# A hybrid decoder step on one core: three edits around the token mixer, and the inner norm sums in two rounded parts

## The chip, the cores and the metric

The kernel runs on one core of a Trainium2 chip. The metric is the device time in microseconds (us) of one execution. Before the change the median of three runs is 2332.24 us (2332.10 to 2332.31).

## What is computed

One decoder layer over 256 prompt tokens and 8 x 4 = 32 sample tokens, 288 columns together, with 2048 features. Everything is float32.

```
h = h + 1/2 SwiGLU(RMSNorm(h))                      # FFN 1, 5632 hidden features
h = h + W_out [ norm(conv group) | norm(attention group) ]
h = h + 1/2 SwiGLU(RMSNorm(h))                      # FFN 2
h = h + sigmoid(W_g RMSNorm(h)) * (W_p p)           # per-layer embedding
y = RMSNorm(h)
attention: softmax(q k^T / sqrt(d) + F_t - F_s, causal) v,  F = running sum of log sigmoid(w_f x + b_f)
```

Attention has 8 heads of 128. The sample tokens attend to 1024 past tokens each, read from a paged cache through a table, and to the new tokens of their own sequence; F runs on over past and new tokens.

## The kernel before

**Products.** The residual `h` lies transposed in SBUF, 128 features by 288 tokens a tile, 16 tiles. A product of float32 quality is made of three products in float32r: the activation is split into a rounded part and the rest (`xh`, `xl`, made by `x_split` and `make_x` through `split`, L194: ScalarE rounds, L195, VectorE subtracts, L196), the weights as well (`whi`, `wlo`, `split_upto`, L263: ScalarE L271, VectorE L272), and TensorE adds hi x hi, hi x lo and lo x hi in one bank of PSUM (`pair`, lines 304, 305, 306). A chunk (a piece of a `pair`) is 512 KB of weights, split in two halves, and 24 products of 128 x 288. The pool of split halves holds five (`HALVES`), the pool of raw weights eight (`RAW`).

**Order.** The source writes a list of steps. A scheduler in the language's layer then chooses the order in which each engine gets its instructions; some are pinned with `keep_in_program_order`. Each engine takes its instructions from its list, one after the other. Weights are loaded on SP's queue (L234 to L237), the cache's pages on POOL's. `defer(fn, chunks)` puts work on a list that is run in the middle of a chunk, so many chunks later.

**Start.** The first two `pair`s (gate and up of FFN 1) are interleaved chunk by chunk, and `first` (L426) splits the activations just ahead of them: features 0, 1, then 2, 3, then 4 to 7 and so on. The loads stand in this order on SP: activations 0 and 1, the first gate weights in two parts, activations 2 and 3, the first up weights, and so on alternately; behind all 16 activation tiles and four gate and four up chunks comes `consts` (L471), which holds among others the identity, masks and the matrix `mean` (all entries 1/2048).

**Norms.** The squares of `h` are added in `acc` (L209 to L215). `norm_scale` (L190) defers `inv_rms` (L175), which multiplies `mean` by `acc` on TensorE in plain float32 (L180), so that each partition holds the mean, and makes the inverse root on ScalarE and VectorE. It is used six times: behind FFN 1's first chunks, for the mixer, for the two groups of the mixer, for FFN 2 and for the embedding; `finish` calls `inv_rms` once more at the end.

**Running sums of the new tokens.** `f_natural` (L555) turns the log forget values. `f_new` (L566) makes the running sums of the 32 new tokens from two products (L568, L569), `f_turn` turns them (L576), `f_rows` (L581) spreads them to 128 rows by a product (L583); each is deferred by a chunk.

**Sample attention.** `k_scores` (L667) is a unit of 16 small products on column tiles (L684); there are 16 units, one every three pieces. `new_scores` (L695) makes the scores of the new tokens, 16 products of 32 columns for each half of the sequences (L699). The pieces are numbered by `at` (L952): unit n stands at 1 + 3n, the two `new_scores` at 20 and 21. `sample_out` (L750) sums the value products of one half under a mask on VectorE (L762, L764) and defers `sample_turn` (L767) by two chunks, which transposes the sum on TensorE (L770).

Of the kernel before, what the change touches and what calls it, by code (L numbers as in the profile page):

```python
# [16 lines left out]
F32 = mybir.dt.float32  # L17
F32R = mybir.dt.float32r
I32 = mybir.dt.int32
AF = mybir.ActivationFunctionType  # L20
ALU = mybir.AluOpType
# [4 lines left out]
P = 128  # L26
# [4 lines left out]
DT = 4  # L31
NS = DB * DT
NT = SEQ + NS
DFF = 5632
NH = 8
# [26 lines left out]
def constants():  # L62

    rows = np.arange(P)
    hc, b, half, t = rows // 32, rows % 32 // 8, rows % 8 // 4, rows % 4
    h = 4 * half + hc
    parts = []

    def put(name, a):
        a = np.asarray(a, np.float32)  # L70
        full = np.zeros((P, a.shape[1]), np.float32)
        full[: a.shape[0]] = a
        at = sum(x.shape[1] for x in parts)
        CONST_COLS[name] = (a.shape[0], at, at + a.shape[1])
        parts.append(full)

    put("ident", np.eye(P))
    put("ones", np.ones((P, 1)))
    put("mean", np.full((P, P), 1.0 / D))
    put("iota", rows[:, None])  # L80
    put("headmask", (rows % 8 // 4 * 4 + rows % 32 // 8)[:, None] == np.arange(NH)[None])
    put("tri", np.where(np.arange(P)[None] <= rows[:, None], 0.0, NEG))
    cb, ct = np.arange(NS) // DT, np.arange(NS) % DT
    for g in range(2):
        own = (cb[None] == (b + 4 * g)[:, None])
        put(f"newmask{g}", np.where(own & (ct[None] <= t[:, None]), 0.0, NEG))
        put(f"newself{g}", own & (ct[None] == t[:, None]))
    put("fold", rows[:, None] % 32 == np.arange(NH)[None])
    put("tri32", (cb[:, None] == cb[None]) & (ct[:, None] <= ct[None]))
    pb, pg = np.arange(64) // PAGES, np.arange(64) % PAGES  # L90
    put("tri64", (pb[:, None] == pb[None]) & (pg[:, None] < pg[None]))
    put("sel64", pb[:, None] == cb[None])
    put("headsel", np.arange(NH)[:, None] == h[None])
    return np.concatenate(parts, 1)


def build(nc, tc, ctx, A, O):
# [3 lines left out]
    v, s, g, pe, sy = nc.vector, nc.scalar, nc.gpsimd, nc.tensor, nc.sync  # L101

    cst = pool("cst")
# [14 lines left out]
    def ktbank():  # L118

        names = [n for n in spare["tags"] for _ in range(BANKS[n])]  # L120
        spare["at"] += 1
        n = names[spare["at"] % len(names)]
        return bank(n, BANKS[n])
# [5 lines left out]
    def const(name):  # L129
        r, a, b = CONST_COLS[name]  # L130
        return C[:r, a:b]
# [7 lines left out]
    at = 0  # L139
# [32 lines left out]
    def log_tables():  # L172
        tc.keep_in_program_order(s.preload_act_table_set("natural_log_exp_and_others"))

    def inv_rms(out, parts, width, load=True):  # L175

        b = ktbank()
        m = b[:, :NT]
        for i, x in enumerate(parts):
            pe.matmul(m, const("mean"), x, start=i == 0, stop=i == len(parts) - 1)  # L180
        if load:
            log_tables()
        c = float(D // width)
        s.activation(ra, m, AF.Ln, bias=eps, scale=c)
        s.activation(out, ra, AF.Exp, scale=-0.5)
        v.scalar_tensor_tensor(ra, out, -0.5 * c, out, ALU.mult, ALU.mult)
        v.scalar_tensor_tensor(ra, m, EPS / c, ra, ALU.add, ALU.mult)
        v.scalar_tensor_tensor(out, ra, 1.5, out, ALU.add, ALU.mult)

    def norm_scale(out, squares, width, chunks):  # L190

        defer(lambda: inv_rms(out, [squares], width), chunks)

    def split(hi, lo, x, gcol):  # L194
        return (s.activation(hi, x, AF.Copy, scale=gcol),  # L195
# [138 lines left out]
    def defer(fn, chunks=1):  # L334

        deferred.append((state["chunk"] + chunks, fn))
# [132 lines left out]
        load_upto(2 * c + 2)  # L469
    items.clear()  # L470
    tc.keep_in_program_order(sy.dma_start(C, A["consts"]))  # L471


    M = {}
# [80 lines left out]
    def f_natural(lf, FT):  # L555
        fp = W["fp"][0]
        np_ = ktbank()
        nat = cst.tile([P, 40], F32, name="nat")
        for j in range(2):
            pe.transpose(np_[:, 16 + j * NH:16 + j * NH + NH], FT[:, j * P:j * P + P], ident[:NH, :NH])  # L560
        pe.transpose(np_[:NS, 32:40], lf[:, SEQ:], ident[:NH, :NH])
        v.tensor_copy(nat[:, 16:32], np_[:, 16:32])
        v.tensor_copy(nat[:NS, 32:40], np_[:NS, 32:40])
        M["nat"] = nat

        def f_new():  # L566
            pn = ktbank()
            pe.matmul(pn[:NS, :NH], const("tri32"), nat[:NS, 32:40], start=True, stop=False)  # L568
            pe.matmul(pn[:NS, :NH], const("sel64"), M["tot"], start=False, stop=True)  # L569
            Fn = fp.tile([NS, NH], F32, name="Fn")  # L570
            v.tensor_copy(Fn, pn[:NS, :NH])
            defer(lambda: f_turn(Fn))

        def f_turn(Fn):
            pt = ktbank()
            pe.transpose(pt[:NH, :NS], Fn, ident[:NS, :NS])  # L576
            FnT = fp.tile([NH, NS], F32, name="FnT")
            v.tensor_copy(FnT, pt[:NH, :NS])
            defer(lambda: f_rows(FnT))

        def f_rows(FnT):  # L581
            px = ktbank()
            pe.matmul(px[:, :NS], const("headsel"), FnT, start=True, stop=True)  # L583
            Fx = fp.tile([P, NS], F32, name="Fx")
            v.tensor_copy(Fx, px[:, :NS])
            M["newbias"], M["Fq"] = [], []
            for gi in range(2):
                nb = cst.tile([P, NS], F32, name=f"nbias{gi}")
                v.tensor_tensor(nb, const(f"newmask{gi}"), Fx, ALU.subtract)
                d = fp.tile([P, NS], F32, name=f"fd{gi}")  # L590
                v.tensor_tensor(d, Fx, const(f"newself{gi}"), ALU.mult)
                fq = cst.tile([P, 1], F32, name=f"fq{gi}")
                v.tensor_reduce(fq, d, AX.X, ALU.add)
                M["newbias"].append(nb)
                M["Fq"].append(fq)

        defer(f_new)
# [97 lines left out]
    def new_scores(gi):  # L695
        sc = ktbank()
        for half in range(2):
            for c in range(4):
                pe.matmul(sc[32 * c:32 * c + 32, :NS], M["qn"][gi][:, 4 * half + c, :], k_[4 * half + c][:, SEQ:],  # L699
                          start=half == 0, stop=half == 1, tile_position=(0, 32 * c))  # L700
        v.scalar_tensor_tensor(M["s", gi][:, PAGES * P:], sc[:, :NS], M["Fq"][gi], M["newbias"][gi], ALU.add, ALU.add)
# [48 lines left out]
    def sample_out(gi):  # L750
        mx = W["vv"][0]
        for b in range(4):
            for e in range(2):
                rows = slice(NS * e, NS * e + NS)
                pe.matmul(M["va", gi][e][32 * b:32 * b + 32, :], M["pv", gi][rows, 8, b], M["vs"][rows], start=False, stop=True,
                          tile_position=(NS * e, 32 * b))
        o = mx.tile([P, P], F32, name="so", tag="so", bufs=2)
        for hh in range(NH):
            src = M["va", gi][hh // 4][:, hh % 4 * P:hh % 4 * P + P]
            m = const("headmask")[:, hh:hh + 1]  # L760
            if hh == 0:
                v.tensor_scalar(o, src, m, None, ALU.mult)  # L762
            else:
                v.scalar_tensor_tensor(o, src, m, o, ALU.mult, ALU.add)  # L764
        defer(lambda: sample_turn(gi, o), 2)

    def sample_turn(gi, o):  # L767
        mx = W["vv"][0]
        t = ktbank()
        pe.transpose(t[:, :P], o, ident)  # L770
        for half in range(2):
            v.tensor_copy(M["oS"][:, 4 * half:4 * half + 4, 16 * gi:16 * gi + 16].rearrange("p c (b t) -> p c b t", t=DT),
                          t[:, :P].rearrange("p (b c a t) -> p a c b t", c=4, a=2, t=DT)[:, half])
        if gi == 1:
            s.dma_start(O["v_prompt"].rearrange("(j p) c -> p j c", p=P), M["vn"])
            for e in range(2):
                s.dma_start(O["v_sample"][:, 512 * e:512 * e + 512], M["vs"][NS * e:NS * e + NS])
            for hh in range(NH):
                split(za[hh][0][:, SEQ:], za[hh][1][:, SEQ:], M["oS"][:, hh, :], gain("norm_attn_out", hh))
            sq = mx.tile([P, NH, NS], F32, name="sqS")  # L780
            s.activation(sq, M["oS"], AF.Square)
            v.tensor_reduce(acc[:, SEQ:], sq.rearrange("p h n -> p n h"), AX.X, ALU.add)
# [169 lines left out]
    def at(i, *fns):  # L952
        marks.setdefault(i, []).extend(fns)
# [31 lines left out]
        fill += pair(A["w_out"], ob * 256, list(range(8)), lambda k: zc[k], out_conv(ob), late=1 if ob == 0 else 0)  # L985
    for n in range(16):
        at(1 + KSTEP * n, units[n] if n > 1 else units[n][1])
    at(20, lambda: new_scores(0))
    at(21, lambda: new_scores(1))
    at(27, lambda: softmax(0))  # L990
    at(49, lambda: softmax(1))
    at(48, v_start)
# [144 lines left out]
```

## Time and profile before

| | |
|---|---|
| median of the runs shown | 2332.24 us |
| span of the profiled execution, first to last instruction (its own time is not listed apart) | 2332.0 us |
| instructions in it | 44271 |
| VectorE busy | 57% |
| ScalarE busy | 45% |
| mean DMA rate | 190 GB/s |
| granted TensorE clock, mean | 0.998 |

In the rows of the profile PE is TensorE's products, PEld its weight loads, DVE VectorE, ACT ScalarE, POOL GpSimd, SP SyncE, and a q behind a name is the engine's sequencer. A timeline row gives the start in us, the length in us, engine, line, operation, output <- inputs, count, and in brackets how long the engine was idle before it and what ended that. Consecutive like instructions are merged in a row. Each float32 product of L180, and most others in float32, stands as two records. Matmul ends are modelled and overlap the next one's start, so spacing is read from starts.

### The profile page before, as it was taken

The page shows a single profiled execution, that of the slowest core. Times are in us where ns is not written, and L with a number is a line of the kernel's source. Part 1 is how long each engine was busy: PE and PEld are TensorE (multiplying, and loading weights), DVE is VectorE, ACT ScalarE, POOL GpSimd, SP SyncE. Part 2 cuts the span into 40 slices and gives each one's busy share as a digit, 9 for nine tenths or more (in the row PEclk, how much of TensorE's full clock was granted, in tenths as well). Part 3 has the DMA queues.
Part 4 walks back from the last instruction along what each step waited for, and adds up shares of the span by engine and source line. Part 5 has one row for each costly group of instructions (what it writes and reads, how often), then busy time and mean ns, then how long its engine had stood idle before and what let it go on. Part 6 is the DMA issues. An engine that isn't in the chain of part 4 may idle for free.

```text
span 2332.0 us, 44271 instructions
## 1 busy us (share of the span) xinstructions
PE 2316.4 (99%) x17390; PEld 2254.6 (97%) x17390; DVE 1338.6 (57%) x2395; ACT 1056.0 (45%) x1859; POOL 328.2 (14%) x401
## 2 busy tenths in 40 slices
PE   9999999999999999999999999999999999999997
PEld 9999999999999999888888999999999999999997
DVE  6555555555555575456466765555555555555755
ACT  7444444444444453334345554444434444444654
POOL 2010000000000013444445210000000000000110
PEclk9999999999999999999999999999999999999999
DMA  8575555545555457998988554545555555555452
GB/s 272 162 241 163 165 169 164 164 164 167 167 163 163 163 161 224 333 313 268 322 306 296 167 165 154 174 158 175 163 164 164 170 163 163 164 167 167 161 169 88
DMA packets 391137, 443.52 MB, mean 190 GB/s; under 512 B 17120, under 2 KB 371824, under 8 KB 390928
## 3 DMA queue, kind: packets, MB, share of 16 engines
q1 hardware_dynamic: 369456, 366.89, 49.3%
q0 software_dynamic: 20384, 71.38, 8.8%
q8 instruction: 136, 2.23, 0.4%
q10 hardware_dynamic: 1088, 2.42, 0.3%
q14 instruction: 73, 0.60, 0.1%
HBM read 435.56 MB, written 5.07 MB: 189 GB/s over the span
## 4 chain that ended last, share of the span: by engine, by line
PE 99%; DVE 0%; DMA 0%; ACT 0%; SPq 0%; issue 0%; DVEq 0%
PE mm L304 31%; PE mm L306 31%; PE mm L305 30%; PE va L742 1%; PE va L684 1%; PE va L304 1%; PE va L306 1%; PE va L305 1%; DMA h<-in_x_dram 0%; DVE h L1072 0%; PE kt L304 0%; PE kt L306 0%; PE kt L305 0%; PE kt L180 0%; PE kt L796 0%; PE kt L829 0%
## 5 line engine op out<-in xcount | busy, mean ns | idle before, releaser
L272 DVE TENSOR_TENSOR wlo<-wraw,whi 128x512 fp32r<-128x512 f32 x1384 | 972.0, 706 | 805.2 <-ACT whi L271 753.2
L271 ACT ACTIVATE whi<-wraw 128x512 fp32r<-128x512 f32 x1384 | 865.3, 630 | 938.5 <-PE mm L305 866.0
L304 PE MATMUL mm<-xh,whi 128*128 128x288 f32 x3680 | 1094.9, 298 | 0.0
L305 PE MATMUL mm<-xl,whi 128*128 128x288 f32 x3680 | 1085.6, 295 | 0.0
L306 PE MATMUL mm<-xh,wlo 128*128 128x288 f32 x3680 | 1082.0, 294 | 0.0
L304 PEld LDWEIGHTS mm<-xh,whi 128*128 128x128 f32 x3680 | 689.7, 187 | 23.2 <-issue 19.4
L306 PEld LDWEIGHTS mm<-xh,wlo 128*128 128x128 f32 x3680 | 692.9, 188 | 0.1
L305 PEld LDWEIGHTS mm<-xl,whi 128*128 128x128 f32 x3680 | 691.0, 188 | 0.2
L304 PE MATMUL mm<-hh,whi 128*128 128x288 f32 x1408 | 416.8, 296 | 0.0
L305 PE MATMUL mm<-hl,whi 128*128 128x288 f32 x1408 | 415.4, 295 | 0.0
L306 PE MATMUL mm<-hh,wlo 128*128 128x288 f32 x1408 | 414.0, 294 | 0.0
L370 POOL TENSOR_TENSOR sr<-sg,rs 128x288 f32<-128x288 f32 x88 | 72.3, 822 | 1409.2 <-ACT sg L368 1409.1
L306 PEld LDWEIGHTS mm<-hh,wlo 128*128 128x128 f32 x1408 | 265.2, 188 | 0.0
L305 PEld LDWEIGHTS mm<-hl,whi 128*128 128x128 f32 x1408 | 264.4, 188 | 0.0
L304 PEld LDWEIGHTS mm<-hh,whi 128*128 128x128 f32 x1408 | 263.8, 187 | 0.0
L390 DVE SCALAR_TENSOR_TENSOR h<-mm,h 128x288 f32<-128x288 f32 x192 | 87.1, 455 | 23.4 <-PE mm L306 23.0
L215 POOL TENSOR_TENSOR acc<-acc,sq 128x288 f32<-128x288 f32 x59 | 51.0, 865 | 248.5 <-ACT sq L214 245.6
L368 ACT ACTIVATE sg<-tg 128x288 f32<-128x288 f32 x88 | 39.1, 444 | 99.9 <-DVE tg L366 96.7
L243 POOL DMA_INDIRECT KT<-in_cache_k_dram,idx x64 | 65.0, 1015 | 122.9 <-PE va L684 54.6
L377 ACT ACTIVATE hh<-hd 128x288 fp32r<-128x288 f32 x88 | 39.2, 446 | 92.8 <-DVE hd L375 92.8
L247 POOL DMA_INDIRECT page<-in_cache_v_dram,idx x64 | 64.7, 1010 | 72.6 <-PE va L742 50.6
L378 DVE TENSOR_TENSOR hl<-hd,hh 128x288 fp32r<-128x288 f32 x88 | 40.7, 464 | 22.0 <-ACT hh L377 22.0
(231 smaller groups left out, 1319.4 us busy)
## 6 DMA issues: line engine op xcount, KB each, us to landing
wraw<-in_w_ffn_up_dram SPq DMA_DIRECT2D x176, 512.0 KB
wraw<-in_w_ffn_gate_dram SPq DMA_DIRECT2D x175, 512.0 KB
wraw<-in_w_ffn_down_dram SPq DMA_DIRECT2D x160, 512.0 KB
wraw<-in_w_in_dram SPq DMA_DIRECT2D x96, 512.0 KB
wraw<-in_w_out_dram SPq DMA_DIRECT2D x32, 512.0 KB
wraw<-in_w_ple_gate_dram SPq DMA_DIRECT2D x32, 512.0 KB
wraw<-in_w_ffn_down_dram SPq DMA_DIRECT2D x32, 256.0 KB
wraw<-in_w_ple_proj_dram SPq DMA_DIRECT2D x8, 256.0 KB
```

The source lines that it names most:

```text
L215: (v if k >= KT - last_on_v else g).tensor_tensor(acc, acc, sq, ALU.add)
L243: g.indirect_dma_start(out=t[:, i].rearrange("p h s -> p (h s)"), out_offset=None, in_=it["src"], in_offset=bass.IndirectOffsetOnAxis(ap=r ...
L247: g.indirect_dma_start(out=t, out_offset=None, in_=it["src"], in_offset=bass.IndirectOffsetOnAxis(ap=it["rows"], axis=0))
L271: s.activation(hi, x, AF.Copy)
L272: v.tensor_tensor(lo, x, hi.bitcast(F32), ALU.subtract)
L304: pe.matmul(o, hi[:, j % 2, w], xh, start=f, stop=False)
L305: pe.matmul(o, hi[:, j % 2, w], xl, start=False, stop=False)
L306: pe.matmul(o, lo[:, j % 2, w], xh, start=False, stop=l)
L370: g.tensor_tensor(r, u, rs, ALU.mult)
L377: s.activation(H["hi"][:, k, :], t, AF.Copy)
L378: v.tensor_tensor(H["lo"][:, k, :], t, H["hi"][:, k, :].bitcast(F32), ALU.subtract)
L390: v.scalar_tensor_tensor(h[:, k, :], o, 0.5, h[:, k, :], ALU.mult, ALU.add)
```

## The change

1. `sample_turn` of the first half is deferred by four chunks instead of two.
2. Both `new_scores` stand at piece 22, behind key unit 7 (1 + 3 x 7 = 22).
3. The new tokens' running sums and their spreading become one product: the totals of the past pages and the new tokens' values are written, spread to 128 columns, in one tile `E` of 96 rows (four VectorE copies), and multiplied by one constant matrix `newsum` of 96 x 32. Three matrices go out of `consts`, which shrinks from 786 to 626 columns.
4. `norm_scale` rounds the sum of squares on ScalarE (`sqh`), makes the rest on VectorE (`sql`) and defers two float32r products with `meanr`, a rounded copy of `mean`. The copy is made once, by a VectorE instruction that stands in the source behind the load of `consts`. The last norm, in `finish`, is as before.

```diff
+    meanr = cst.tile([P, P], F32R, name="meanr")
+    sqh, sql = (cst.tile([P, NT], F32R, name=f"sq{x}") for x in "hl")
+
-    def inv_rms(out, parts, width, load=True):
+    def inv_rms(out, parts, width, load=True, weights=const("mean")):
...
-            pe.matmul(m, const("mean"), x, start=i == 0, stop=i == len(parts) - 1)
+            pe.matmul(m, weights, x, start=i == 0, stop=i == len(parts) - 1)
...
     def norm_scale(out, squares, width, chunks):
-        defer(lambda: inv_rms(out, [squares], width), chunks)
+        s.activation(sqh, squares, AF.Copy)
+        v.tensor_tensor(sql, squares, sqh.bitcast(F32), ALU.subtract)
+        defer(lambda: inv_rms(out, [sqh, sql], width, weights=meanr), chunks)
...
     tc.keep_in_program_order(sy.dma_start(C, A["consts"]))
+    v.tensor_copy(meanr, const("mean"))
...
+        def spread(rows, src):
+            for a in range(2):
+                v.tensor_copy(E[rows].rearrange("p (c b a t) -> p c b a t", c=4, b=4, a=2)[:, :, :, a],
+                              src[:, 4 * a:4 * a + 4].unsqueeze(2).unsqueeze(3).to_broadcast([src.shape[0], 4, 4, DT]))
+        E = fp.tile([96, P], F32, name="sums")
+        spread(slice(0, 64), M["tot"])
+        spread(slice(64, 96), nat[:NS, 32:40])
         def f_new():
-            pn = ktbank()
-            pe.matmul(pn[:NS, :NH], const("tri32"), nat[:NS, 32:40], start=True, stop=False)
-            pe.matmul(pn[:NS, :NH], const("sel64"), M["tot"], start=False, stop=True)
-            Fn = fp.tile([NS, NH], F32, name="Fn")
-            v.tensor_copy(Fn, pn[:NS, :NH])
-            defer(lambda: f_turn(Fn))
-        def f_turn(Fn):
...
-        def f_rows(FnT):
             px = ktbank()
-            pe.matmul(px[:, :NS], const("headsel"), FnT, start=True, stop=True)
+            pe.matmul(px[:, :NS], E, const("newsum"), start=True, stop=True)
...
-        defer(lambda: sample_turn(gi, o), 2)
+        defer(lambda: sample_turn(gi, o), 4 if gi == 0 else 2)
...
-    at(20, lambda: new_scores(0))
-    at(21, lambda: new_scores(1))
+    at(22, lambda: new_scores(0), lambda: new_scores(1))
```

More of the change, by code (lines that the diff above doesn't have):

```diff
@@ L64, in constants @@
     rows = np.arange(P)
-    hc, b, half, t = rows // 32, rows % 32 // 8, rows % 8 // 4, rows % 4
-    h = 4 * half + hc
+    b, t = rows % 32 // 8, rows % 4
     parts = []
@@ L88, in constants @@
     put("fold", rows[:, None] % 32 == np.arange(NH)[None])
-    put("tri32", (cb[:, None] == cb[None]) & (ct[:, None] <= ct[None]))
     pb, pg = np.arange(64) // PAGES, np.arange(64) % PAGES
     put("tri64", (pb[:, None] == pb[None]) & (pg[:, None] < pg[None]))
-    put("sel64", pb[:, None] == cb[None])
-    put("headsel", np.arange(NH)[:, None] == h[None])
+    put("newsum", np.concatenate([pb[:, None] == cb[None], (cb[:, None] == cb[None]) & (ct[:, None] <= ct[None])]))
     return np.concatenate(parts, 1)
@@ L564, in f_natural @@
         M["nat"] = nat
-        def f_new():
-            pn = ktbank()
-            pe.matmul(pn[:NS, :NH], const("tri32"), nat[:NS, 32:40], start=True, stop=False)
-            pe.matmul(pn[:NS, :NH], const("sel64"), M["tot"], start=False, stop=True)
-            Fn = fp.tile([NS, NH], F32, name="Fn")
-            v.tensor_copy(Fn, pn[:NS, :NH])
-            defer(lambda: f_turn(Fn))
-        def f_turn(Fn):
[L575 to L579, printed above, removed]
-        def f_rows(FnT):
+        def spread(rows, src):
[5 more added lines that the diff above has]
+        spread(slice(64, 96), nat[:NS, 32:40])
+        def f_new():
             px = ktbank()
-            pe.matmul(px[:, :NS], const("headsel"), FnT, start=True, stop=True)
+            pe.matmul(px[:, :NS], E, const("newsum"), start=True, stop=True)
             Fx = fp.tile([P, NS], F32, name="Fx")
```

## The prediction, on record before the run

> **What bounds the kernel now.** I read the page first, then the waits of PE, then timelines where the change cuts in.
>
> ```profile
> span 2332.0 us, 44271 instructions
> ...
> PE 2316.4 (99%) x17390; PEld 2254.6 (97%) x17390; DVE 1338.6 (57%) x2395; ACT 1056.0 (45%) x1859; POOL 328.2 (14%) x401
> ```
>
> ```profile
> PE mm L461 <- DVE acc L458: 1.3, 1, 1.3
> PE kt L770 <- DVE pst L812: 1.3, 1, 1.3
> ```
>
> TensorE never rests, and of its few waits only one is touched by the edits: L770, 1.3 us. So a saving must be PE time or that wait, and whatever holds PE anywhere is paid in full.
>
> PE's own price of a small product is read from starts of the products around it:
>
> ```profile
> 987.01 0.29 PE L306 MATMUL mm<-xh,wlo 128*128 128x288 f32 x1
> ...
> 987.41 0.29 PE L306 MATMUL mm<-xh,wlo 128*128 128x288 f32 x1
> ...
> 988.13 0.30 PE L305 MATMUL mm<-xl,whi 128*128 128x288 f32 x1
> ```
>
> From 987.01 to 987.41 there are three steps: 0.133 us a product. From 987.41 to 988.13 stand two steps (0.27) and the 16 products of L699: they cost 0.72 - 0.27 = 0.45 us. The same reading serves L180, L568 with L569, L576 and L583:
>
> ```profile
> 37.25 0.29 PE L306 MATMUL mm<-xh,wlo 128*128 128x288 f32 x1
> 37.38 0.65 PE L180 MATMUL kt<-acc,consts 128*128 128x288 f32 x2
> ...
> 38.00 0.29 PE L305 MATMUL mm<-xl,whi 128*128 128x288 f32 x1
> ```
>
> ```profile
> 886.94 0.29 PE L306 MATMUL mm<-xh,wlo 128*128 128x288 f32 x1
> ...
> 887.71 0.30 PE L305 MATMUL mm<-xl,whi 128*128 128x288 f32 x1
> ```
>
> ```profile
> 890.64 0.29 PE L306 MATMUL mm<-xh,wlo 128*128 128x288 f32 x1
> ...
> 891.22 0.29 PE L305 MATMUL mm<-xl,whi 128*128 128x288 f32 x1
> ```
>
> ```profile
> 894.15 0.29 PE L306 MATMUL mm<-xh,wlo 128*128 128x288 f32 x1
> ...
> 894.95 0.30 PE L305 MATMUL mm<-xl,whi 128*128 128x288 f32 x1
> ```
>
> L180 costs 0.75 - 0.27 = 0.48 us, the sums 0.77 - 0.27 = 0.50, the turn 0.58 - 0.27 = 0.31, the spreading 0.80 - 0.27 = 0.53.
>
> **What the four edits save on PE.** (1) The wait at L770 goes, 1.3 us; two pieces later (about 6 us) VectorE has long written the sum. (2) Two `new_scores` cost 0.90. Behind a unit of like products they need no change of mode of their own; I count 0.15 each, since most of the 0.45 is the change from and to the float32r stream, and save 0.6 (ends 0 and 0.8). (3) Three groups, 0.50 + 0.31 + 0.53 = 1.34, become one of the shape of L583, 0.53: 0.8 saved (ends 0.5 and 1.1). (4) A norm's product becomes two of 0.133: 0.48 - 0.27 = 0.21, six times 1.3 (ends 0 and 1.6, if a change of type still costs, or not). Together 4.0 us; if only the wait and half of (3) came, 1.7; all upper ends, 4.8. The four copies and the new `sqh`, `sql` (0.45 us each by the rows of like size, below) lie on VectorE and ScalarE, which the page shows at 57% and 45%.
>
> ```profile
> L215 DVE TENSOR_TENSOR acc<-acc,sq 128x288 f32<-128x288 f32 x14 | 6.3, 454 | 1.1 <-POOL acc L215 0.7
> ```
>
> They lengthen each norm's chain by about 1 us ahead of PE's product. Tightest is the first norm: `acc` is complete at 36.94 (35.93 + 1.01 below), the product starts at 37.38.
>
> ```profile
> 35.93 1.01 DVE L215 TENSOR_TENSOR acc<-acc,sq 128x288 f32<-128x288 f32 x2
> ```
>
> That would make PE wait up to 0.6 us, if the start stayed as it is. It doesn't.
>
> **What the copy of `mean` does at the start.** The copy needs `consts`, and the order of the changed program shows where the scheduler put it on VectorE:
>
> ```
> before: xl 0,1 | wlo x2 | xl 2,3 | wlo x2 | xl 4-7 | wlo ...
> after:  wlo x2 | xl 2,3 | wlo x2 | xl 4-7 | wlo | meanr <- consts | xl 0,1 | wlo ...
> ```
>
> The copy stands thirteenth, and `xl` of features 0 and 1 stand behind it. PE's order changes little: four hi x hi products of feature 0, then the first product with `xl` of feature 0, the fifth. So PE waits from its fifth product until `consts` has landed and VectorE has made the copy and `xl` 0. ScalarE can't go round: its sixth half of weights needs a place that PE frees.
>
> When does `consts` land? In the timeline of before it is issued late:
>
> ```profile
> 5.11 0.95 DVE L196 SCALAR_TENSOR_TENSOR xl<-h,gT,xh 128x288 fp32r<-128x288 f32 x2 [3.91 <-ACT xh L195]
> ...
> 11.08 1.81 DVE L196 SCALAR_TENSOR_TENSOR xl<-h,gT,xh 128x288 fp32r<-128x288 f32 x4
> 12.88 2.61 DVE L272 TENSOR_TENSOR wlo<-wraw,whi 128x512 fp32r<-128x512 f32 x4
> ```
>
> ```profile
> 13.18 2.22 SPq L471 DMA_DIRECT2D consts<-in_consts_dram  x1
> ```
>
> and behind 6400 KB of activations and weights, at a full DMA:
>
> ```profile
> 0.00:5.00 5.00, 3.74 (x8) 2.71 (x9) 0.36 (x2) 1.74 (x3) 1.91 (x8) 1.00 0.64 192
> 5.00:10.00 5.00, 4.69 (x26) 3.60 (x26) 3.47 (x7) 3.54 (x8) 0.00 (x0) 1.00 1.01 344
> 10.00:15.00 5.00, 5.00 (x40) 5.00 (x40) 4.92 (x10) 4.29 (x10) 0.00 (x0) 1.00 1.07 374
> 15.00:20.00 5.00, 5.00 (x40) 5.00 (x39) 4.56 (x9) 4.37 (x9) 0.00 (x0) 1.00 1.07 368
> 20.00:25.00 5.00, 5.00 (x40) 5.00 (x39) 3.46 (x7) 4.16 (x11) 1.38 (x2) 1.00 1.08 361
> ```
>
> The last number is GB/s: 0.96 MB by 5 us, 2.68 by 10, 4.55 by 15, 6.39 by 20. Queue order puts ahead of the end of `consts`: gains and state 124 KB, activations 2304, weights 4096, `consts` itself 393: 6917 KB, 7.08 MB, moved at 21.9 us. A load lands somewhat behind that count:
>
> ```profile
> consts<-in_consts_dram SPq DMA_DIRECT2D x1, 393.0 KB
> ```
>
> ```profile
> 10.51 1.82 ACT L195 ACTIVATE xh<-h,gT 128x288 fp32r<-128x288 f32 x4 [0.30 <-DMA h<-in_x_dram]
> ...
> 14.93 1.82 ACT L195 ACTIVATE xh<-h,gT 128x288 fp32r<-128x288 f32 x4 [0.25 <-DMA h<-in_x_dram]
> ```
>
> These two waited for their loads; by the count (2300 and 3900 KB) those were moved at 9.1 and 13.5 us, so they landed 1.4 us behind it. In the changed kernel `consts` is 80 KB smaller, 0.2 us. That gives 23.1 us as the early end. The lag can be twice that where five loads are under way behind it: 24.5, the late end. I take 24.2, nearer the late one, because the queue is at its deepest there (DMA share 1.08). None of the loads ahead of it waits for VectorE, so the wait doesn't move it.
>
> VectorE's copy is bounded by a 128 x 128 operation,
>
> ```profile
> L487 DVE TENSOR_TENSOR wg<-wf,gT 128x128 f32<-128x128 f32 x1 | 0.3, 286 | 0.0
> ```
>
> 0.3 us, and `xl` 0 takes half of 0.95: PE goes on at 24.2 + 0.3 + 0.5 = 25.0. In before:
>
> ```profile
> 6.08 0.40 PE L304 MATMUL va<-xh,whi 128*128 128x288 f32 x1
> ...
> 10.23 0.29 PE L304 MATMUL kt<-xh,whi 128*128 128x288 f32 x1
> ```
>
> the first chunk's 24 products ended at 10.23, from where PE runs on without a gap; counted back at 0.133 that is a gapless start at 7.04. In the changed kernel four products are done early, so 25.0 stands for a gapless start at 24.5. **The hold costs 17.4 us** (16.4 to 17.8 by the two landings).
>
> After it the five split halves and all early loads are there. SP's third load behind `consts` waits for a half that VectorE splits only after the hold, at about 30 us; it is used by chunk 10, beyond 50 us: hidden. The squares have lost their wait for the last activations, so the first norm should come earlier against PE than before, and its 0.6 us is not counted.
>
> **The clock.** PE idles some 15 us, and the clock falls at idle:
>
> ```profile
> L461 PE MATMUL mm<-acc 128*128 128x288 f32 x10 | 5.0, 683 | 1.3 <-DVE acc L458 1.3
> ```
>
> ```profile
> 2320.00:2324.00 4.00, 0.08 (x1) 0.00 (x0) 2.77 (x6) 0.94 (x2) 0.00 (x0) 0.95 0.01 3
> 2324.00:2328.00 4.00, 0.00 (x0) 0.00 (x0) 4.00 (x6) 0.00 (x0) 0.00 (x0) 0.50 0.93 350
> ```
>
> PEclk (third from the end) is 0.95 in the four us around PE's last product, which ends 0.08 into them, and 0.50 in the next: it falls to half (1 - 2 x 0.05) x 4 = 3.6 us into the stretch, some 3.5 us behind that product. At the start ten passes of 288 columns took 5.0 us, 0.5 each, where the two of L180 take 0.24 each: half clock; the first products behind them already run at 0.133. So the restart is slow for up to 4.8 us and loses half of that: **2.4 us** (ends 0, if the clock held, and 3.6, if it takes two stretches as long as that of the fall). The Trainium skill, TensorE: Matmul & The Clock Gate, section "What's actually happening", says that the clock halves after an idle window of about 3.4 us, and comes back after one busy window that runs free of the kernel. By it the restart would lose between 1.7 and 3.4 us, an estimate from that page alone; the 3.6 us of the profile's end agree.
>
> **Sum.** 17.4 + 2.4 - 4.0 = +15.8 us. The profiled span is 2332.0, the median 2332.24; the 0.2 us between them is kept. **2332.2 + 15.8 = 2348.0 us.**
>
> **Rivals.**
> - *The clock stays up over the gap*: 17.4 - 4.0, 2345.6 us. For it: the page's slices show no fall. Against it: the last rows above.
> - *More is lost behind the hold*: ScalarE's and VectorE's queues, stopped for 11 us, come back in a new order with four squares in a row, and the chains of the norms are 1 us longer; a missed half costs PE about 0.7 us each (a split of weights), two to five of them 1.4 to 3.5 us: 2349.4 to 2351.5.
> - *Not slower: the copy holds nothing that PE needs*, and the change does what it says. Then only the savings are left: 2332.2 - 4.0 = 2328.2 us. It decides at `xl` 0: PE loses less than 4.0 us if that is written by 11.5 us (7.04 + 4.0 + 4 x 0.133). For it only that the order could be another on the chip; against it 6400 KB ahead of `consts`, which is issued at 13.18, later than that.
> - A landing at once would still leave `xl` 0 behind `xl` 4 to 7 and a `wlo`, that is at 13.5 + 0.8 = 14.3 us in place of 5.6: 14.3 - 0.5 - 7.0 - 4.0 = +2.8 us, 2335.0.
>
> **Chances.** Forecast within its own terms 0.75, clock stays 0.10, more lost 0.09, not slower 0.04, early landing 0.02. The range runs from the low ends (16.4 + 0 - 4.8 = +11.6, 2343.8) to the high ones (17.8 + 3.6 - 1.7 = +19.7, 2351.9): 2343.8 to 2351.9 us. What a measurement can tell here is about 0.2%, 4.7 us: faster than 2327.6 0.02, between 0.04 (the other half of the third rival and the fourth), slower than 2336.9 0.94.
>
> **What would show it.** In the profile of the changed kernel: VectorE's copy of `mean` at L474 idle for about 11 us behind DMA `consts`, at 23 to 25 us; the DMA rate in the first 20 us as before; PE waiting about 15 us for `xl` before a product at about 25 us, then products spaced at 0.24 to 0.27 for 3 to 7 us; L770 without a wait; a gap of 0.27 in place of 0.48 at the norms; from 60 us on every stage at the same distance from before, about 19 us later, and 4 us less at the end. Wrong would be: a copy that starts early, or PE busy between 10 and 24 us.

## The result, and the profile after

| | before | after |
|---|---|---|
| median of five runs each, measured together | 2332.30 us (2332.10 to 2332.46) | 2346.56 us (2345.99 to 2347.17) |
| span of the profiled execution | 2332.0 us | 2345.4 us |
| mean granted clock | 0.998 | 0.994 |

The changed kernel is 14.3 us slower: a ratio of 1.0061, with a 95% interval of 1.0051 to 1.0072. 2348.0 had been forecast.

The page of the changed kernel, its span, busy times and the two rows of slices that differ from a steady picture:

```profile
span 2345.4 us, 44277 instructions
...
PE 2315.0 (99%) x17385; PEld 2255.6 (96%) x17385; DVE 1344.3 (57%) x2404; ACT 1058.8 (45%) x1865; POOL 329.4 (14%) x401
...
PE   6999999999999999999999999999999999999997
...
PEclk8999999999999999999999999999999999999999
```

PE's busy time has even gone down by 1.4 us. What is new is in the first of the 40 slices: a 6 for PE and an 8 for its clock, where before had a 9 in both. The waits of PE say what happened there (total, times and longest, in us):

```profile
PE va L307 <- DVE xl L198: 12.6, 1, 12.6
PE kt L306 <- ACT whi L273: 3.2, 1, 3.2
...
PE kt L180 <- ACT sq L1051: 0.7, 1, 0.7
```

L770's wait (now L768) is gone, and one of 12.6 us has come in. The 3.2 us are part of the same gap: they stand between the four products that PE can do early, the last two of which start at 9.71. The 0.7 us stand ahead of the last norm. The timeline of VectorE and then that of PE, from 12 us on:

```profile
12.80 0.69 DVE L274 TENSOR_TENSOR wlo<-wraw,whi 128x512 fp32r<-128x512 f32 x1
22.17 0.23 DVE L474 CAST meanr<-consts 128x128 fp32r<-128x128 f32 x1 [8.68 <-DMA consts<-in_consts_dram]
22.32 0.94 DVE L198 SCALAR_TENSOR_TENSOR xl<-h,gT,xh 128x288 fp32r<-128x288 f32 x2
```

```profile
9.71 0.53 PE L306 MATMUL kt<-xh,whi 128*128 128x288 f32 x2 [3.21 <-ACT whi L273]
22.88 0.61 PE L307 MATMUL va<-xl,whi 128*128 128x288 f32 x1 [12.63 <-DVE xl L198]
23.29 0.44 PE L308 MATMUL va<-xh,wlo 128*128 128x288 f32 x1
...
27.61 0.44 PE L306 MATMUL va<-xh,whi 128*128 128x288 f32 x1
...
28.07 0.30 PE L308 MATMUL va<-xh,wlo 128*128 128x288 f32 x1
28.21 0.29 PE L307 MATMUL kt<-xl,whi 128*128 128x288 f32 x1
```

VectorE stands idle for 8.68 us in front of the copy of `mean`, whose data have not landed. `xl` 0, behind it, waits for nothing else (it follows at 22.32 without a pause), and PE needs it. When PE goes on at 22.88 its products start 0.24 us apart; from 28.07 on they are 0.13 apart. The windows carry the clock (third from the end) and the DMA rate (last):

```profile
0.00:5.00 5.00, 3.74 (x10) 2.76 (x10) 0.36 (x2) 1.83 (x3) 1.92 (x8) 1.00 0.62 186
5.00:10.00 5.00, 1.18 (x6) 0.58 (x4) 2.55 (x5) 3.37 (x7) 0.00 (x0) 1.00 1.01 334
10.00:15.00 5.00, 0.25 (x2) 0.01 (x1) 3.48 (x7) 2.52 (x6) 0.00 (x0) 0.60 1.07 395
15.00:20.00 5.00, 0.00 (x0) 0.00 (x0) 0.00 (x0) 0.00 (x0) 0.00 (x0) 0.50 1.07 396
20.00:25.00 5.00, 2.12 (x9) 2.12 (x10) 1.08 (x3) 0.00 (x0) 0.00 (x0) 0.50 0.83 299
25.00:30.00 5.00, 5.00 (x29) 5.00 (x29) 1.75 (x4) 2.35 (x5) 0.00 (x0) 0.70 0.08 15
```

From 15 to 20 us no compute engine does anything. The rest of the kernel gives some of the loss back; the products' starts show how much. The first norm, and the one product of the running sums:

```profile
55.00 0.29 PE L308 MATMUL mm<-xh,wlo 128*128 128x288 f32 x1
55.13 0.30 PE L180 MATMUL kt<-sqh,meanr 128*128 128x288 f32 x1
55.27 0.29 PE L180 MATMUL kt<-sql,meanr 128*128 128x288 f32 x1
55.40 0.29 PE L306 MATMUL mm<-xh,whi 128*128 128x288 f32 x1
...
904.27 0.29 PE L308 MATMUL mm<-xh,wlo 128*128 128x288 f32 x1
904.40 0.31 PE L581 MATMUL kt<-consts,sums 96*128 96x32 f32 x2
...
904.76 0.29 PE L307 MATMUL mm<-xl,whi 128*128 128x288 f32 x1
```

The first norm stands at 55.13 instead of 37.38: 17.75 us late, which is the whole loss of the start. The norm's two products take 0.27 us instead of 0.48. The sums take 904.76 - 904.27 - 2 x 0.133 = 0.22 us in place of 1.34. A key unit without and the one with the new tokens' scores behind it:

```profile
998.37 0.29 PE L308 MATMUL mm<-xh,wlo 128*128 128x288 f32 x1
998.59 1.92 PE L682 MATMUL va<-KT,strip 128*32 128x512 f32 x16
...
1000.68 0.29 PE L307 MATMUL mm<-xl,whi 128*128 128x288 f32 x1
...
1010.01 0.29 PE L308 MATMUL mm<-xh,wlo 128*128 128x288 f32 x1
...
1011.98 0.48 PE L697 MATMUL kt<-k,qn 128*32 128x32 f32 x32
1012.39 0.40 PE L306 MATMUL mm<-xh,whi 128*128 128x288 f32 x1
1012.62 0.30 PE L307 MATMUL mm<-xl,whi 128*128 128x288 f32 x1
```

2.31 us and 2.61 us: the 32 products cost 0.30 us there, 0.90 before.

The loads of the weights (PEld) show where the new sums differ from L583, which is a float32 product of 32 columns too; first L583 in before, then the new product:

```profile
894.38 0.29 PEld L583 LDWEIGHTS kt<-FnT,consts 8*128 8x128 f32 x2 [0.17 <-issue]
```

```profile
904.27 0.32 PEld L581 LDWEIGHTS kt<-consts,sums 96*128 96x128 f32 x2
```

The new weights are loaded from 904.27 on, while the product ahead of them runs; those of L583 only after 0.17 us of rest, and so are those of L568, L576 and L699. These four load 8 x 128, 32 x 32, 32 x 8 and 128 x 32 weights, a part of the 128 x 128 array; the float32 norms (128 x 128) have no such rest either. So in these traces the rest goes with the shape and not with float32; no run varies the shape alone. Last, the norm at the end, which the change doesn't touch, first in the timeline of before and then in that of after:

```profile
2318.77 1.31 PE L180 MATMUL kt<-sq,consts 128*128 128x288 f32 x3
```

```profile
2332.25 1.31 PE L180 MATMUL kt<-sq,consts 128*128 128x288 f32 x3
```

13.48 us late: of 17.75 lost at the start 4.27 are given back, by norms 6 x 0.21 = 1.26, sums 1.12, scores 0.60, and the turn with the remainder, 1.29, about its wait.

### The profile page after: what moved, and what is told of

Read it like the earlier page. It is cut to its first block, busy times and chain, and to the rows that moved or that the text cites. A ratio compares the mean times of both kernels' runs of the same rounds, so it can differ in the third digit from the quotient of the medians.

```text
span 2345.4 us, 44277 instructions
## 1 busy us (share of the span) xinstructions
PE 2315.0 (99%) x17385; PEld 2255.6 (96%) x17385; DVE 1344.3 (57%) x2404; ACT 1058.8 (45%) x1865; POOL 329.4 (14%) x401
## 4 chain that ended last, share of the span: by engine, by line
PE 98%; DMA 1%; SPq 0%; DVE 0%; ACT 0%; issue 0%; DVEq 0%
PE mm L306 31%; PE mm L308 30%; PE mm L307 30%; PE va L740 1%; PE va L682 1%; PE va L307 1%; PE va L308 1%; PE va L306 1%; DMA consts<-in_consts_dram 0%; DVE h L1069 0%; SPq L239 0%; PE kt L308 0%; PE kt L307 0%; PE kt L306 0%; DMA gT<-in_gains_dram 0%; PE kt L794 0%
## 5 line engine op out<-in xcount | busy, mean ns | idle before, releaser
L306 PEld LDWEIGHTS mm<-xh,whi 128*128 128x128 f32 x3680 | 689.7, 187 | 22.2 <-issue 19.4
```

Of the source, the lines that this page charges most:

```text
L306: pe.matmul(o, hi[:, j % 2, w], xh, start=f, stop=False)
```

## The experiments

The theory was: the whole loss comes from one VectorE instruction, the copy of `mean`, that stands ahead of the split halves in an in-order queue while its load is far down SP's queue; then the clock restarts at half. The rivals: that the edits themselves cost time, or that the added instruction costs by its place, whatever its data.

**The copy alone, on the kernel before.** Nothing reads `meanr` in this kernel.

```diff
+    meanr = cst.tile([P, P], F32R, name="meanr")
...
     tc.keep_in_program_order(sy.dma_start(C, A["consts"]))
+    v.tensor_copy(meanr, const("mean"))
```

> The kernel before, and only the copy of mean added behind the load of the constants; nothing reads it. Theory: PE waits for xl 0 as in the changed kernel; the constants are 80 KB larger, 0.2 us later: 17.9 us more, 2350.2 us, plus what of the changed kernel's extra 1.5 us outside the span belongs to the hold, up to 2351.7. Rival (norms or other edits): an unused copy costs 0.2 us on an engine at 57%: 2332.5 us.

Measured 2351.10 us (2350.63 to 2351.74) beside 2332.21 for before, ratio 1.0081 with an interval of 1.0065 to 1.0096: what the theory gave. VectorE and the first wait of PE:

```profile
24.26 0.23 DVE L473 CAST meanr<-consts 128x128 fp32r<-128x128 f32 x1 [9.77 <-DMA consts<-in_consts_dram]
```

```profile
PE va L306 <- DVE xl L197: 13.5, 1, 13.5
```

One instruction of 0.23 us that serves nothing costs 18.9 us. This is more than the change as a whole, because the edits' savings (2.7 us, next run) are missing and the load lands 2 us later (24.26 instead of 22.17).

**The changed kernel with the copy later in VectorE's queue.** It is written into the seventh step of the interleaved start, behind that step's squares.

```diff
             if c >= 4:
                 x_squares(c - 4)
+            if c == 6:
+                v.tensor_copy(meanr, const("mean"))
...
     tc.keep_in_program_order(sy.dma_start(C, A["consts"]))
-    v.tensor_copy(meanr, const("mean"))
```

> All four edits, but the copy of mean is written into the seventh interleaved chunk of the start, so that VectorE's order has xl 0 and 1 first again and the copy behind all xl. Theory (the copy's place in VectorE's order holds PE: 17.7 us; the edits save 4.3): the start as before, 2332.3 - 4.3 = 2328.0 us, no PE wait over 1.3 us. Rival (the loss lies in the norms made of two parts, or in the other edits): the time stays near 2346.5 us.

Measured 2329.50 us (2328.69 to 2330.20), ratio 0.9989, interval 0.9980 to 0.9998. The copy by its tile:

```profile
L446 DVE CAST meanr<-consts x1: 831/831/831, 24.1 to 24.1; 128x128 fp32r<-128x128 f32 x1
```

It starts at 24.1 us, and the long wait of PE is gone, so the rival falls. The same four edits are now 2.7 us faster than before. The theory had 4.3 and 2328.0 us; the 1.5 us that are missing are taken up below, at the turn.

**The copy on GpSimd**, at its old place in the source.

```diff
-    v.tensor_copy(meanr, const("mean"))
+    g.tensor_copy(meanr, const("mean"))
```

> All four edits, the copy of mean at the same place of the source but on GpSimd. It waits for the same load, until about 22 us. Theory (what counts is who stands behind the copy): GpSimd's first sum of squares starts at about 25 us, so nothing waits: 2328.0 us, as with the late copy. Rival (the load of the constants itself, or its use, slows the start): 2340 us or more.

Measured 2329.49 us (2328.93 to 2329.78), ratio 0.9988, interval 0.9979 to 0.9997.

```profile
22.69 2.16 POOL L217 TENSOR_TENSOR acc<-acc,sq 128x288 f32<-128x288 f32 x2 [19.73 <-ACT sq L216]
24.80 0.75 POOL L474 CAST meanr<-consts 128x128 fp32r<-128x128 f32 x1
25.52 5.00 POOL L217 TENSOR_TENSOR acc<-acc,sq 128x288 f32<-128x288 f32 x5
```

The copy had been expected to wait for its load, and it didn't. It stands behind GpSimd's first two sums of squares, which wait for ScalarE until 22.69; the constants were issued at 13.1 and landed 9.5 us later, at 22.6. The run shows that the copy costs nothing off VectorE's queue and behind work that starts later than its load lands. It doesn't show what a waiting copy costs on an engine with nothing queued behind it.

**The constants loaded first.** The copy keeps its engine and its place in the source. The scheduler then puts it ahead of all split halves on VectorE.

```diff
+    tc.keep_in_program_order(sy.dma_start(C, A["consts"]))
     for c in range(4):
         x_load(4 * c
...
     items.clear()
-    tc.keep_in_program_order(sy.dma_start(C, A["consts"]))
     v.tensor_copy(meanr, const("mean"))
```

> The changed kernel with the load of the constants issued first on SP, ahead of all activations and weights; VectorE's copy of mean then stands first in its queue, ahead of every split half. Theory A (the time went because the copy waits in VectorE's queue for a load that lands at 22 us; with an early landing nothing is held): the constants, 320 KB, push all later loads back by 0.8 us at 395 GB/s, and the copy itself costs 0.2 us, so 2329.5 (the time with the late copy) + 1.0 = 2330.5 us, range 2329.5 to 2332.0; PE starts about 1 us later and has no wait of more than 2 us. Rival B (a foreign instruction in VectorE's first splits costs the start by its place, whenever its data land): 2335 us or more, with a wait of PE for xl of over 4 us.

Measured 2329.56 us (2329.22 to 2332.29) beside 2332.24 for before, ratio 0.9990, interval 0.9981 to 0.9999. VectorE and PE in its timeline:

```profile
3.92 0.23 DVE L474 CAST meanr<-consts 128x128 fp32r<-128x128 f32 x1 [2.72 <-DMA consts<-in_consts_dram]
5.45 0.95 DVE L198 SCALAR_TENSOR_TENSOR xl<-h,gT,xh 128x288 fp32r<-128x288 f32 x2 [1.30 <-ACT xh L197]
```

```profile
6.64 0.40 PE L306 MATMUL va<-xh,whi 128*128 128x288 f32 x1 [0.74 <-ACT whi L273]
```

The second rival falls: foremost in the queue, but with its data there at 3.9 us, the copy holds nothing. Beside the changed kernel, where the copy stands ahead of `xl` 0 and its data come at 22.17, this shows that the cost needs both, the place and the late data. The expected loss of 1 us for the earlier 320 KB did not show (2329.56 against 2329.40 for the late copy beside it). PE's first product with split weights is 0.66 us later than in the changed kernel (5.98).

**The edits without the norms' parts**: no copy, no `meanr`, and `norm_scale` as before; the other three edits stay.

```diff
-        s.activation(sqh, squares, AF.Copy)
-        v.tensor_tensor(sql, squares, sqh.bitcast(F32), ALU.subtract)
-        defer(lambda: inv_rms(out, [sqh, sql], width, weights=meanr), chunks)
+        defer(lambda: inv_rms(out, [squares], width), chunks)
...
-    v.tensor_copy(meanr, const("mean"))
```

> The later turn, the new tokens' scores behind the key unit and the sums in one product; the norms as before, no copy. Theory: by the stages of the two profiles the turn saves 1.4 us, the scores 0.6, the sums 1.1: 2332.3 - 3.1 = 2329.2 us; against the late copy this leaves 1.2 us for the six norms. Rival (the norms in parts save nothing): the same time as the late copy.

Measured 2330.58 us (2330.07 to 2331.31), ratio 0.9993, interval 0.9984 to 1.0003: 1.63 us below before, and not the 3.1 expected. The interval holds 1, but every run of this kernel is below every one of before (2331.71 to 2333.49). The sums and scores of the trace are 1.72, so nothing is left for the turn. The late copy is 1.08 below this, against the rival; the norms' own rows gave 1.26.

**Before, a second time, and the turn alone.** Both before and the kernel with the copy alone have the turn at two pieces; the first trace shows PE's wait ahead of it, the second does not. So before was profiled again, beside before with the turn's edit only.

```diff
-        defer(lambda: sample_turn(gi, o), 2)
+        defer(lambda: sample_turn(gi, o), 4 if gi == 0 else 2)
```

> The kernel before, unchanged, profiled once more: its first profile had a span of 2332.0 us, while the runs of it in the last comparison have spans around 2330.4. Theory A (the 1.3 us wait of the first half's turn was there in the profiled execution and is not in most): a span near 2330.4 and no PE wait for the turn. Theory B (the wait is there each time, and the 1.6 us come from elsewhere): the wait again, 1.3 us, and another part shorter.

> The kernel before with the later turn alone. Theory A (the wait is not in most executions): within 0.2 us of the kernel before, 2332.2. Theory B (it is there each time): 1.4 us less, 2330.8.

On this chip before had 2333.62 us (2333.15 to 2334.07); taken again 2333.58, and with the turn's edit 2332.36 (2331.77 to 2332.82), ratio 0.9994, interval 0.9985 to 1.0003. The second profile of before has the wait:

```profile
PE kt L770 <- DVE pst L812: 1.2, 1, 1.2
```

With the edit it is gone, and 1.26 us with it; the interval holds 1, but the runs of the two don't overlap. The medians of before differ from one comparison to the other by about that much (2332.2 to 2332.3 in three, 2333.6 in this one). That fits a wait that is there on one chip and not on another, which neither expectation had said; no profile of plain before was taken in a comparison where it ran at 2332.2.

The rows of ScalarE and VectorE ahead of the turn, in the first trace of before, show where the wait comes from:

```profile
1190.64 0.63 ACT L271 ACTIVATE whi<-wraw 128x512 fp32r<-128x512 f32 x1 [1.42 <-PE mm L306]
1191.31 0.69 DVE L272 TENSOR_TENSOR wlo<-wraw,whi 128x512 fp32r<-128x512 f32 x1 [1.39 <-ACT whi L271]
1191.92 0.34 DVE L764 SCALAR_TENSOR_TENSOR so<-va,consts,so 128x128 f32<-128x128 f32 x1
```

The last addition of the sum (L764) stands on VectorE behind a split of weights, which waits for ScalarE, which is itself idle for 1.42 us. The kernel with the copy alone has the same order on both engines there, and in its trace ScalarE makes this half without a pause. Of the 13 profiles five have this pause, of 1.35 to 1.42 us: the first of before and all four of this comparison (before again, the turn alone, and the kernels with more warming products and with wide constants, below). The eight others have none; seven of them come from two other chips, and for that of the changed kernel the chip is not on record. So the pause goes with the chip and not with the program, or with the comparison, for each ran on one chip. What it waits for is open.

**The late copy with the turn back at two pieces**, beside the late copy once more.

```diff
-        defer(lambda: sample_turn(gi, o), 4 if gi == 0 else 2)
+        defer(lambda: sample_turn(gi, o), 2)
```

> The late copy with the turn of the first half's value sums back at two pieces, beside the late copy itself on one chip. Theory A (the turn's edit is worth the wait at the turn, and nothing else): where the profile of this kernel shows PE waiting for the sum ahead of the turn, the time is above that of copy_late_b by about that wait (1.2 us); where it shows none, the two agree within 0.4 us. Rival B (two pieces later saves or costs something of its own, whether the wait is there or not): a difference of 0.5 us or more without a wait, or none with it.

> The late copy once more, for the two others to stand beside. Theory A (its gain is the four edits' own: 0.6 for the scores, 1.1 for the sums, 1.1 for the norms, and 1.3 for the turn where the kernel before waits there): below the kernel before by 2.8 us where before runs at about 2332.2 on this chip, by 4.0 us where it runs at about 2333.6. Rival B (the gain is the same on every chip): 2.7 us below before either way.

Measured 2329.39 us (2329.01 to 2329.80) with the turn back and 2329.40 (2329.03 to 2330.16) without, before 2332.24. The trace with the turn back has no wait there, as the first theory has it, so the edit is worth nothing on this chip: its two extra pieces neither cost nor save. Whether the wait comes back where before has it wasn't tried. The late copy is 2.84 us below before; 2.8 was expected for a chip without the wait, and 2.7 by the rival, so this tells nothing between them.

**More warming products.** The kernel begins with products on zeros; 38 in place of 5 keep PE at work while VectorE waits.

```diff
-WARM = 5
+WARM = 38
```

> The changed kernel, with 38 idle float32 products at the start in place of 5, so that PE is busy (10 passes slow, then 66 of 0.24 us) until about 21.8 us, that is until the constants land. Theory (the clock falls over the gap and costs the restart 2.4 us): products at 0.133 us right after the hold, 2346.6 - 2.4 = 2344.2 us. Rival (the slow products come from something else than the gap): 2346.6 us. If the four early products, queued behind the idle ones, end later than the hold, 0.5 us more.

Measured 2345.12 us (2344.94 to 2345.77), ratio 1.0049, interval 1.0034 to 1.0065. PE in its timeline:

```profile
22.88 0.40 PE L307 MATMUL va<-xl,whi 128*128 128x288 f32 x1 [0.60 <-DVE xl L198]
23.12 0.30 PE L308 MATMUL va<-xh,wlo 128*128 128x288 f32 x1
...
25.91 0.30 PE L307 MATMUL kt<-xl,whi 128*128 128x288 f32 x1
```

It goes on at the same 22.88, but at full speed: 25.91 instead of 28.21, 2.3 us. That is the size that the theory gives to the clock; its time, 2344.2, was missed by 0.9 us. Of the 2.3 us, 2.0 are left at the last norm and in the spans: 0.3 are lost near 1020 us, for a reason that isn't settled. In the medians 1.4 are left (2346.56 - 2345.12), which come from different comparisons: the changed kernel's profiled execution was the longest of its five, 0.6 us above its median, and that of the warmed kernel 0.1 above its own.

**Wide constants.** 160 columns of zeros that nothing reads bring the constants of the changed kernel back to 786 columns.

```diff
+    put("pad", np.zeros((P, 160)))
     put("newsum", np.concatenate(
```

> The changed kernel with 160 unused columns in the constants, 786 in all as in the kernel before. The changed kernel's constants landed for VectorE at 22.2 us with the DMA at 395 GB/s between 10 and 20 us; where the constants were 786 columns wide they came at 24.3, with 366 to 374 GB/s, though most of the loads are the same. Theory A (the width goes with the rate of all loads): the copy at about 24.3 us, 2346.6 + 2.1 = 2348.7 us. Theory B (the rate differs from one execution to the next): the copy at 22.2 + 0.2 us, 2346.8 us.

Measured 2348.12 us (2347.94 to 2348.48), ratio 1.0062, interval 1.0047 to 1.0077: 1.56 us above the changed kernel, nearer to theory A.

```profile
L475 DVE CAST meanr<-consts x1: 227/227/227, 23.3 to 23.3; 128x128 fp32r<-128x128 f32 x1
```

```profile
10.00:15.00 5.00, 0.56 (x2) 0.21 (x1) 3.47 (x7) 2.51 (x6) 0.00 (x0) 0.50 1.08 370
15.00:20.00 5.00, 0.00 (x0) 0.00 (x0) 0.00 (x0) 0.00 (x0) 0.00 (x0) 0.50 1.08 366
```

The copy is 1.1 us later than in the changed kernel and than in the warmed one, which ran on the same chip (22.17 in both), and the DMA rate is back at 370 and 366 GB/s, well before the constants themselves move. The spans are 0.9 us apart; the rest of the 1.56 is again the changed kernel's profiled execution. The 24.3 us of the theory were not reached. So the changed kernel's third edit, which dropped three matrices, also made its hold shorter.

## Why the prediction was right, point by point

- **The order on VectorE and what it holds**: right, and shown (the copy is the twelfth behind VectorE's two memsets, not the thirteenth, which changes nothing). The copy alone costs 18.9 us (its own hold, reckoned as below, is 24.97 - 4 x 0.133 - 7.04 = 17.4 us), and three ways to get it out of the way (later, on another engine, its data earlier) all give 2329.4 to 2329.6.
- **The hold, 17.4 us**: right in mechanism, 2 us too long. PE went on at 22.88 with the fifth product; counted like the prediction's 25.0 that is 22.88 - 4 x 0.133 - 7.04 = 15.3 us. The step that was mis-sized is the landing, taken at 24.2 us near the late end; it came at 22.2, below the early end of 23.1. Two parts of it: the windows above give 6.56 MB by 20 us, so that the 7.0 MB are moved at 21.1 and not at 21.7; and the load landed 1.1 us behind the count, where 2.5 had been taken. The sign "the DMA rate in the first 20 us as before" failed with it: 395 and 396 GB/s where before has 374 and 368. With wide constants the landing was at 24.26 in one kernel, as taken, and at 23.32 in the other, 2.5 and 1.4 us behind the count; so the lag is no fixed figure, and no run says what sets it.
- **The clock, 2.4 us**: right in size at its place. PE ran at half clock from 22.88 until 28.0; 5.1 us of products at 0.24 that need 0.133 lose 2.3, and the warmed kernel shows the same 2.3. That it came within 0.1 is luck in part: the slow stretch was taken as at most 4.8 us, and in the two other kernels with a hold it was 4.0 us (copy alone, 24.97 to 28.97) and 4.7 (wide constants, 24.03 to 28.73). The Trainium skill, TensorE: Matmul & The Clock Gate, section "What's actually happening", has the clock come back after one busy window of about 3.4 us that doesn't start with the kernel; the 5.1, 4.0 and 4.7 us here lie between one such window and two, which agrees. The rival "the clock stays up" gave 2345.6, nearer to the measured 2346.56 than the forecast; the time alone would have spoken for it, and the trace speaks against it.
- **The savings, 4.0 us**: 4.27 in the two profiles. Norms 0.21 each, as counted; scores 0.60, as counted; sums 1.12 instead of 0.8, since the new product cost 0.22 and not the 0.53 of L583. The step that failed there is the reason given for the price of the small products, the change from and to float32r: the new product is plain float32 as well, and the loads of the weights above show no rest ahead of it. It has another shape on the array than L583. In the medians of the comparison with the late copy only 2.7 to 2.8 arrive: the turn's 1.3 us is a wait, and with the sums, scores and norms 2.98 the experiments fit an execution of before that doesn't have it.
- **The 0.2 us between span and median**: wrong. Every run lies about 1.8 us above its own span (2347.17 and 2345.4; 2332.34 and 2330.6 in a run of before). The profiled execution of before, with a span of 2332.0, therefore was, by this rule, one of some 2333.8 us, 1.5 above the median (the second profile of before has 2331.8 and 2333.58). Added to the span of after less its own 0.6, this joins the two differences: 13.4 + 1.5 - 0.6 = 14.3.
- **No wait at the first norm, nothing more lost behind the hold**: right. Behind 30 us PE's only wait in its list of waits is the 0.7 us ahead of the last norm, which before has too, and the distance to before shrinks from 17.75 at the first norm to 13.48 at the last.

Together: for the profiled execution 2332.0 + 15.8 = 2347.8 us had been worked out, and its span is 2345.4, 2.4 less, of which 2.05 are the start and 0.27 the savings. From there to the median 0.2 us had been added and 1.16 were needed (2346.56 - 2345.4), which takes 0.96 of the error back, by luck, and leaves 1.4.

## What to carry to other kernels

On an engine that takes its instructions in order, one small instruction that needs a late load holds all that a scheduler has put behind it: look where it stands in the built order of that engine, and count when its data land. If nothing needs its result soon, put it behind the urgent work, or on another engine behind work that starts later, or load its data first; here each of the three turned 14.3 us lost into 2.7 to 2.8 us gained. And before a saving is taken from a wait in one profiled execution, see whether a second profile has it too.

## What the runs showed of the hardware that was not expected

- The DMA rate between 10 and 20 us went with the width of the constants, although these stand behind 6400 KB of other loads: 366 to 374 GB/s in the five profiled executions with 786 columns, 393 to 398 in those with 626, with PE busy or idle alike, and with the constants first in the queue too (393). On two chips both widths were profiled, so it isn't the chip. The kernel with 160 unused columns shows that it is the width or what follows from it (where the tiles or the tensors lie); which of these is open.
- The same program waits 1.2 to 1.3 us at one place on one chip and seemingly not on another, and runs 1.3 us longer there (2333.6 against 2332.2 us). ScalarE's pause ahead of it, 1.35 to 1.42 us, is in all four profiles from one chip, of four different programs, and in none of the seven from two others.
- The 128 x 128 copy stands with 0.23 us on VectorE where the engine was idle before it, with 0.83 us between two splits (the late copy), and with 0.75 us on GpSimd. Why it is longer between the splits was not looked into.
